# Logarithm and scans of the forget gates ordered behind the evictions of the forgetting attention, and spread over one more step of the fill

## The chip, the core and the metric

The kernel runs on one core of a Trainium2 chip. The metric is device time in microseconds (us). TensorE (PE) multiplies, with its weight loads on PEld; VectorE (DVE), ScalarE (ACT) and GpSimd (POOL) work element by element; SyncE (SP) issues most of the transfers.

## The reference

One residual block on a sequence of 1024 rows of 1024 elements, in float32. After a norm and one input projection three mixers run side by side: HGRN2 (a gated linear recurrence, 4 heads with 128 x 128 states), the forgetting attention (8 heads of 64) and cross-attention into a memory. Their outputs are projected, gated, summed and projected again; a ConvGLU channel mixer follows. What the change touches is the decay of the HGRN2 heads:

```python
f = lb + (1.0 - lb) * jax.nn.sigmoid(f_logit.astype(jnp.float32))
kh = heads(1.0 - f)
G = jnp.cumsum(heads(jnp.log(f)), axis=3)      # within chunks of 64 rows
...
o = (jnp.einsum('bhts,bhsv->bhtv', A, ic)      # A: queries, keys and exp of differences of G
     + jnp.einsum('bhtc,bhcv->bhtv', qc * jnp.exp(Gc), S))
```

The forgetting attention, beside which this work runs, is per head and block of 128 queries

```python
s = (jnp.einsum('bhqd,bhkd->bhqk', qh[:, :, lo:hi], kh[:, :, :hi]) * scale
     + Fc[:, :, lo:hi, None] - Fc[:, :, None, :hi])
p = jax.nn.softmax(jnp.where(mask, s, -jnp.inf), axis=-1)
outs.append(jnp.einsum('bhqk,bhkd->bhqd', p, vh[:, :, :hi]))
```

## The kernel before

All large products are run as three matmuls each (`mm3`, lines 110 to 112): high part by high part, low by high, high by low. The projections that the mixers need later are not done in one piece. A generator, `fill_steps()`, deals them out: 18 units of `cm_unit`, each with 7 yields (products of sums of blocks, so that 7 products stand for 8), and 24 chunks of the branch projections behind them. Six steps run alone, and then the generator is woven with the eight heads of the forgetting attention (`fox_attn(h)`, about 330 to 690 us, with 2, 6 and then 5 steps of the fill to a head, `FOX_FILL`), with the four HGRN heads (`hgrn_mix(h)`), and the rest runs out behind them. The fill gives PE work while the attention waits for its softmax.

A unit of the fill loads weights into `ur` (SP, L798), forms sums `us` on POOL (L738), casts them to the high part `uh` on ACT (L732), takes the low part `ul` on DVE (L733), multiplies into `pp`, copies results out on ACT (`ue`, L743), combines them on DVE (`ue` and `uo`, L136, L138, L784) with activations on ACT (L763, L773, L776, L783), and stores to DRAM.

A head of the attention has four groups `tp`. Each takes two blocks of queries: logits `lg` by PE (L1029, L1030), a masked sum with a row maximum on DVE (L1035), the negated maximum (L1042), exp on ACT (L1045), reciprocal on DVE (L1046), scaling on POOL (L1047). Then PE transposes the probabilities into `tr` (L1058 to L1061), they are split into `ph` (a cast on ACT, L116) and `pl` (a subtraction on DVE, L124), and PE multiplies them with the values into `po` (L1070, L1071). `po` is emptied by a copy of its upper half on ACT (`yp`, L1074) and an add of the lower half on DVE (L1075), and `yp` is stored (L1076). There are 32 such evictions. The next head's inputs (`kh`, `qa`, `kl`, `nf`, `vhl`: L999 to L1005, on SP) are loaded behind the first `yp` store of the head before.

`decays(h)` makes the decays of HGRN head `h`: load of the gate into `fk` (SP, L949), two tensor_scalars on DVE (L952, L953), the logarithm of 128 x 2048 elements on ACT (L955), with a load of its table ahead of it and of exp's or tanh's table again ahead of the next activation, four scans (L958) and four subtractions (L959) of 128 x 256 on DVE, and two stores (L962, SP). `fk` has one buffer, so a load waits for the stores of the head before. `fill_steps` calls it in units 1, 2, 4 and 5: the load at step 2, all the computation at step 4, the stores at step 6.

What sets the order: a scheduler puts the instructions of each engine into one order when the program is built, by priorities and its own estimate of when each can run; the attention's have a priority raised by `AHEAD`. Inside `tc.issue_after(x)` an instruction comes to stand behind instruction `x` in the order of its own engine. That adds no wait; each engine then runs strictly in its order. `marks["cast"]` is the last cast of a `uh` so far, `marks["head"]` the first `yp` store of a head.

Of the kernel before, what the change touches and what calls it, by code (L numbers as in the profile page):

```python
# [12 lines left out]
ALU = mybir.AluOpType  # L13
# [55 lines left out]
def tile_block(ctx: ExitStack, tc: tile.TileContext, xT, x_rows, memT, mem_rows, vec, fbias, mats, hmask, w_ff, w_tm, w_cm,  # L69
               w_mkv, w_br, w_out, w_up, w_dn, outT):  # L70
    nc = tc.nc
    V, S, G, PE, SP = nc.vector, nc.scalar, nc.gpsimd, nc.tensor, nc.sync
# [655 lines left out]
    marks = {}  # L728
# [59 lines left out]
    def cm_unit(u, puts):  # L788

        x, z, y = (banks[(u + i) % 3] for i in range(3))  # L790

        def put(c, n, ps, e):
            puts[c](c, n, ps, e)

        raw = []
        for i in range(4):
            t = ur.tile([P, HB], F32, tag="ur", name="ur", bufs=4)
            SP.dma_start(t, w_cm[u, i])  # L798
            raw.append(t)
        a11, a12, a21, a22 = raw  # L800
        o1, o6 = u_operand(a11), u_operand(a12)
        s1 = u_sum(a21, a22)
        s2 = u_sum(s1, a11)
        u_product(x, o1, "B11", True)
        e1 = u_snap(x)
        yield
        u_product(z, o6, "B21", True)
        put(0, 0, z, e1)
        o3 = u_operand(s2)
        yield  # L810
        u_product(x, o3, "T2", False)
        e2 = u_snap(x)
        o2 = u_operand(s1)
        s4 = u_sum(s2, a12)
        yield
        u_product(y, o2, "T1", True)
        e5 = u_snap(y)
        o5 = u_operand(u_sum(a11, a21))
        yield
        u_product(x, o5, "T3", False)  # L820
        put(1, 1, x, e5)
        o4 = u_operand(s4)
        yield
        u_product(y, o4, "B22", False)
        put(0, 1, y, e2)
        o7 = u_operand(a22)
        yield
        u_product(x, o7, "T4", False)
        put(1, 0, x, None)
        yield  # L830

    def puts_of(what, i):
        return put_gate(i) if what == "gt" else put_hg("fqg".index(what), i)
# [95 lines left out]
    def load_y(br):  # L929
        yr[br] = [fam_tile(("B11", "B22")[ORDER.index(br) % 2], p, (P, 2, T), F32) for p in "hl"]  # L930
        for i, t in enumerate(yr[br]):
            n = 2 if br or i == 0 else 1
            SP.dma_start(t[:, :n, :], yd3[br][:, 2 * i:2 * i + n, :])
# [12 lines left out]
    def decays(h):  # L946

        fk = pf.tile([P, 2, T], F32, tag="fk", name=f"fk_{h}")
        SP.dma_start(fk[:, 0, :], hgd[h][0])  # L949
        yield  # L950
        hc = slice(h, h + 1)
        V.tensor_scalar(fk[:, 1, :], fk[:, 0, :], nc1[:, hc], c1p[:, hc], ALU.mult, ALU.add)  # L952
        V.tensor_scalar(fk[:, 0, :], fk[:, 0, :], c1[:, hc], c0[:, hc], ALU.mult, ALU.add)  # L953
        with tc.issue_after(marks["cast"].ins):
            S.activation(fk, fk, AF.Ln)  # L955
        for n in range(4):
            sl = slice(n * 256, (n + 1) * 256)
            V.tensor_tensor_scan(fk[:, 0, sl], resets, fk[:, 0, sl], 0.0, ALU.mult, ALU.add)  # L958
            V.tensor_sub(fk[:, 1, sl], fk[:, 0, sl], fk[:, 1, sl])  # L959
        yield  # L960
        for i in range(2):
            SP.dma_start(hgd[h][3 + i], fk[:, i, :])  # L962

    def fill_steps():
        for u, spec in enumerate(UNITS):
            for i, _ in enumerate(cm_unit(u, [puts_of(*s) for s in spec])):
                if u == len(UNITS) - 1 and i == 1:
                    load_y(ORDER[0])
                if u == 3 and i == 4:
                    recurrence_masks()  # L970
                if u in (1, 2, 4, 5):
                    if i == 2:
                        steps = decays((1, 2, 4, 5).index(u))
                    if i in (2, 4, 6):
                        next(steps, None)
                yield
        yield from branches()
        ur.release()
# [10 lines left out]
    resets = pf.tile([P, 256], F32, tag="resets", name="resets")  # L989
# [20 lines left out]
    def fox_attn(h):  # L1010
        p, a = h // 2, slice(64 * (h % 2), 64 * (h % 2) + 64)
        with tc.issue_after(marks["head"].ins) if h else nullcontext():
            kh, kl, qa, vhl, nf = fox_load(h)
        for tp in range(4):
            pts = []
            for j in range(2):
                tb = 2 * tp + j
                ns = (tb + 1) * P
                tsl = slice(tb * P, (tb + 1) * P)
                pt = pf.tile([P, T], F32, tag="pt", name="pt", bufs=4)  # L1020
                st = pf.tile([P, 4], F32, tag="st", name="st", bufs=4)
                nfm = pf.tile([P, P], F32, tag="nfm", name="nfm")
                G.tensor_tensor(nfm, nf[tb // 4][:, tb % 4 * P:tb % 4 * P + P], mskf, ALU.add)
                m = 0
                for s0 in range(0, ns, HB):
                    w = min(HB, ns - s0)
                    ps = ps_lg()
                    with tc.issue_after(begun.ins):
                        PE.matmul(ps[:, :w], qa[:, tsl], kh[:, s0:s0 + w], start=True, stop=False)  # L1029
                    PE.matmul(ps[:, :w], qa[:, tsl], kl[:, s0:s0 + w], start=False, stop=True)  # L1030

                    d = w - P if s0 + w == ns else w
                    for lo, hi, bias in ((0, d, nf[s0 // HB][:, :d]), (d, w, nfm)):
                        if lo < hi:
                            V.tensor_tensor_reduce(out=pt[:, s0 + lo:s0 + hi], in0=ps[:, lo:hi], in1=bias,  # L1035
                                                   op0=ALU.add, op1=ALU.max, scale=1.0, scalar=-3e38,
                                                   accum_out=st[:, m:m + 1])
                            m += 1
                if m == 3:
                    V.tensor_tensor(st[:, 0:1], st[:, 0:1], st[:, 2:3], ALU.max)  # L1040
                if m > 1:
                    V.tensor_scalar(st[:, 2:3], st[:, 0:1], st[:, 1:2], -1.0, ALU.max, ALU.mult)  # L1042
                else:
                    V.tensor_scalar(st[:, 2:3], st[:, 0:1], -1.0, None, ALU.mult)
                S.activation(pt[:, :ns], pt[:, :ns], AF.Exp, bias=st[:, 2:3], accum_out=st[:, 3:4])  # L1045
                V.reciprocal(st[:, 3:4], st[:, 3:4])  # L1046
                G.tensor_scalar(pt[:, :ns], pt[:, :ns], st[:, 3:4], 0.0, ALU.mult, ALU.add)  # L1047
                pts.append(pt)
                yield
            po = ps_po()  # L1050
            for sp in range(tp + 1):
                ptr = ps_tr()
                w = 384 if sp == tp else 512
                for jj in range(2):
                    sb = 2 * sp + jj
                    ssl = slice(sb * P, (sb + 1) * P)
                    if sb <= 2 * tp:
                        PE.transpose(ptr[:, jj * 256:jj * 256 + P], pts[0][:, ssl], ident)  # L1058
                        PE.transpose(ptr[:, jj * 256 + P:jj * 256 + 256], pts[1][:, ssl], ident)
                    else:  # L1060
                        PE.transpose(ptr[:, 256:384], pts[1][:, ssl], ident)  # L1061
                ph = pf.tile([P, HB], F32R, tag="ph", name="ph", bufs=2)
                pl = pf.tile([P, HB], F32R, tag="pl", name="pl", bufs=2)
                split(S, ph[:, :w], pl[:, :w], ptr[:, :w])
                for jj in range(2):
                    sb = 2 * sp + jj
                    last = sb == 2 * tp + 1
                    o = po[:, P:256] if last else po[:, 0:256]
                    src = slice(256, 384) if last else slice(jj * 256, jj * 256 + 256)
                    PE.matmul(o, vhl[:, sb, :], ph[:, src], start=(sb == 0), stop=False)  # L1070
                    PE.matmul(o, vhl[:, sb, :], pl[:, src], start=False, stop=last)  # L1071
                yield
            yp = pf.tile([64, 256], F32, tag="yp", name="yp")
            S.copy(yp, po[64:128, :256])  # L1074
            V.tensor_add(yp, po[0:64, :256], yp)  # L1075
            stored = SP.dma_start(yd3[1][a, p, tp * 256:(tp + 1) * 256], yp)  # L1076
            if tp == 0:
                marks["head"] = stored
            yield
# [592 lines left out]
    for a, b, own, first, c, n, sign, last, xq in (  # L1672
# [9 lines left out]
        for i, ks in enumerate(steps):  # L1682
# [11 lines left out]
            for m in range(4):  # L1694
                w = 256 if end and ks.stop == NP and m == 3 else HB
                for t0 in range(0, HB, w):
# [7 lines left out]
                    if ks.stop == NP:  # L1704
                        j, sl = m + 4 * c, slice(n * HB + t0, n * HB + t0 + w)
# [105 lines left out]
```

## Time and profile before

| | |
|---|---|
| runs | 1704.29, 1705.58, 1708.75 us; median 1705.58 |
| profiled execution | 1707.61 us, its span 1705.8 |
| mean granted TensorE clock | 0.992 |
| PE busy | 1673.9 us, 98% of the span |
| DVE, ACT, POOL busy | 1214.6, 844.5, 449.1 us |

A busy PE is the bound almost everywhere, so the profile is read for the few microseconds in which PE stands, what ended each of them, and what that instruction had been queued behind on its own engine. Rows of the trace give the start, the duration, the engine, the line of the kernel, the operation, output <- input, the shape, and in brackets the idle time of the engine just before with what ended it. The four logarithms of the decays start at 340.3, 374.9, 427.5 and 458.8 us.

### The profile page before, as it was taken

How to read it: one execution, taken by the hardware profiler on the slowest of the kernel's cores; microseconds unless marked ns; L12 is line 12 of the kernel's file. 1: busy time of each engine (PE TensorE's matmuls, PEld its weight loads, DVE VectorE, ACT ScalarE, POOL GpSimd, SP SyncE). 2: the span in 40 equal slices, each digit the busy share in tenths (PEclk: the TensorE clock that was granted, in tenths of full speed). 3: DMA queues.
4: the chain of work that ended last, by engine and by line, in shares of the span. 5: the costliest groups of instructions: out<-in, count | busy, mean ns of one | idle time of the engine just before them, and what ended most of it. 6: DMA issues, size and time to landing. Idle time of an engine off the chain costs nothing. (4 is left out here: it accounts for less than half of the span.)

```text
span 1705.8 us, 24936 instructions
## 1 busy us (share of the span) xinstructions
PE 1673.9 (98%) x8883; PEld 1414.9 (83%) x8883; DVE 1214.6 (71%) x2177; ACT 844.5 (50%) x1449; POOL 449.1 (26%) x482
## 2 busy tenths in 40 slices
PE   8999999999899999999999999999999999999999
PEld 5989999778788888888888787888888888788887
DVE  7875765587876666789676667878778777674654
ACT  7745554466666655565332357434444334343331
POOL 0333543565454543222111224211111111100000
PEclk9999999999999999999999999999999999999999
DMA  7353352656555542557858998756345454394772
GB/s 288 111 186 104 126 189 93 227 176 178 182 146 161 149 133 93 189 165 259 281 180 224 282 250 188 220 152 164 117 130 149 135 144 140 138 378 138 258 253 87
DMA packets 134749, 305.54 MB, mean 179 GB/s; under 512 B 14328, under 2 KB 31992, under 8 KB 133984
## 3 DMA queue, kind: packets, MB, share of 16 engines
q1 hardware_dynamic: 101008, 210.87, 36.8%
q0 software_dynamic: 24400, 78.39, 18.3%
q10 hardware_dynamic: 9216, 14.68, 2.4%
q8 instruction: 70, 1.15, 0.3%
q14 instruction: 55, 0.45, 0.1%
HBM read 223.21 MB, written 107.41 MB: 194 GB/s over the span
## 5 line engine op out<-in xcount | busy, mean ns | idle before, releaser
L1348 ACT CAST wh<-s 128x512 fp32r<-128x512 f32 x80 | 48.8, 618 | 120.3 <-PE pp L111 65.2
L116 ACT CAST dwh<-wr 128x1024 fp32r<-128x1024 f32 (+1 forms) x41 | 40.1, 978 | 119.0 <-PE tr L111 40.4
L1348 ACT CAST wh<-rw 128x512 fp32r<-128x512 f32 x70 | 43.1, 620 | 90.0 <-PE pp L111 48.4
L732 ACT CAST uh<-ur 128x512 fp32r<-128x512 f32 x78 | 48.2, 618 | 77.4 <-PE pp L111 65.1
L1473 POOL DMA_DIRECT2D rw<-in_w_up x40 | 22.0, 556 | 199.9 <-DVE wl L1349 151.9
L1047 POOL TENSOR_SCALAR pt<-pt,st 128x128 f32<-128x128 f32 (+3 forms) x64 | 57.2, 895 | 60.0 <-DVE st L1046 42.4
L124 DVE TENSOR_TENSOR dwl<-wr,dwh 128x1024 fp32r<-128x1024 f32 (+1 forms) x41 | 46.3, 1129 | 37.1 <-ACT dwh L116 37.1
L110 PE MATMUL pp<-B21h,uh 128*128 128x512 f32 x168 | 67.0, 400 | 4.1 <-DVE gt L897 2.9
L1045 ACT ACTIVATE pt<-pt,st 128x128 f32<-128x128 f32 (+3 forms) x64 | 49.8, 778 | 40.6 <-DVE st L1042 34.9
L733 DVE TENSOR_TENSOR ul<-us,uh 128x512 fp32r<-128x512 f32 x72 | 54.4, 760 | 17.4 <-ACT uh L732 17.0
L112 PE MATMUL pp<-B21h,ul 128*128 128x512 f32 x168 | 66.5, 396 | 0.1
L111 PE MATMUL pp<-T2l,uh 128*128 128x512 f32 x168 | 66.5, 396 | 0.0
L112 PE MATMUL pp<-T2h,ul 128*128 128x512 f32 x168 | 66.4, 396 | 0.0
L110 PE MATMUL pp<-T2h,uh 128*128 128x512 f32 x168 | 66.4, 399 | 0.0
L111 PE MATMUL pp<-B21l,uh 128*128 128x512 f32 x168 | 66.3, 394 | 0.0
L733 DVE TENSOR_TENSOR ul<-ur,uh 128x512 fp32r<-128x512 f32 x78 | 59.6, 765 | 8.6 <-ACT uh L732 8.6
L738 POOL TENSOR_TENSOR us<-ur 128x512 f32<-128x512 f32 x36 | 49.9, 1386 | 58.3 <-DMA ur<-in_w_cm 49.3
L1349 DVE TENSOR_TENSOR wl<-rw,wh 128x512 fp32r<-128x512 f32 x70 | 46.9, 684 | 20.9 <-PE pp L112 16.7
L738 POOL TENSOR_TENSOR us<-us,ur 128x512 f32<-128x512 f32 x36 | 51.0, 1416 | 40.5 <-issue 34.9
L124 DVE TENSOR_TENSOR wl<-raw,wh 128x1024 fp32r<-128x1024 f32 x29 | 37.1, 1284 | 31.9 <-ACT wh L116 31.7
L732 ACT CAST uh<-us 128x512 fp32r<-128x512 f32 x72 | 43.8, 614 | 32.0 <-POOL us L738 16.1
L1349 DVE TENSOR_TENSOR wl<-s,wh 128x512 fp32r<-128x512 f32 x80 | 54.5, 681 | 0.0
(721 smaller groups left out, 6161.9 us busy)
## 6 DMA issues: line engine op xcount, KB each, us to landing
rw<-in_w_up POOLq DMA_DIRECT2D x40, 512.0 KB, 4.7
ur<-in_w_cm SPq DMA_DIRECT2D x72, 256.0 KB, 3.8
sd<-in_w_dn POOLq DMA_DIRECT2D x30, 512.0 KB, 5.9
br<-yd SPq DMA_DIRECT2D x30, 512.0 KB, 4.7
gd<-uo ACTq DMA_DIRECT2D x48, 256.0 KB, 2.4
gt<-gd SPq DMA_DIRECT2D x48, 256.0 KB, 6.2
yd<-fc SPq DMA_DIRECT2D x44, 256.0 KB, 2.1
raw<-in_w_tm SPq DMA_DIRECT2D x20, 512.0 KB, 3.8
```

Source lines behind the costliest of these rows:

```text
L110: PE.matmul(ps, lh, rh, start=first, stop=False, skip_group_check=more)
L111: PE.matmul(ps, lh, rl, start=False, stop=False, skip_group_check=more)
L112: return PE.matmul(ps, ll, rh, start=False, stop=last, skip_group_check=more)
L116: S.copy(out, in_)
L124: return (sub or V).tensor_sub(l, src, h.bitcast(F32))
L732: marks["cast"] = S.copy(h, src)
L733: V.tensor_sub(l, src, h.bitcast(F32))
L738: G.tensor_add(t, a, b)
L1045: S.activation(pt[:, :ns], pt[:, :ns], AF.Exp, bias=st[:, 2:3], accum_out=st[:, 3:4])
L1047: G.tensor_scalar(pt[:, :ns], pt[:, :ns], st[:, 3:4], 0.0, ALU.mult, ALU.add)
L1348: late["cast"] = S.copy(h, src)
L1349: late["split"] = V.tensor_sub(l, src, h.bitcast(F32))
```

## The change

In `decays` the computation is cut by two more yields: tensor_scalars, then the logarithm with the first two scans and subtractions, then the other two. `fill_steps` now advances it at each step from 2 on, so that the load is at step 2, the tensor_scalars at 3, the logarithm and half of the scans at 4, the other half at 5, the stores at 6. The logarithm is ordered on ACT behind the last copy of `yp` that has been written so far (`marks["out"][0]`) in place of the last cast; the scans and subtractions are ordered on DVE behind the last add of `yp` (`marks["out"][1]`), where nothing held them before. Lines behind the diff's places move by up to 3: the logarithm is L956, scans and subtractions L960 and L961, the stores L965, exp L1048, copy and add of `yp` both L1077, its store L1078.

```diff
@@ decays
         V.tensor_scalar(fk[:, 0, :], fk[:, 0, :], c1[:, hc], c0[:, hc], ALU.mult, ALU.add)
-        with tc.issue_after(marks["cast"].ins):
+        yield
+        with tc.issue_after(marks["out"][0].ins):
             S.activation(fk, fk, AF.Ln)
         for n in range(4):
             sl = slice(n * 256, (n + 1) * 256)
-            V.tensor_tensor_scan(fk[:, 0, sl], resets, fk[:, 0, sl], 0.0, ALU.mult, ALU.add)
-            V.tensor_sub(fk[:, 1, sl], fk[:, 0, sl], fk[:, 1, sl])
-        yield
+            with tc.issue_after(marks["out"][1].ins):
+                V.tensor_tensor_scan(fk[:, 0, sl], resets, fk[:, 0, sl], 0.0, ALU.mult, ALU.add)
+                V.tensor_sub(fk[:, 1, sl], fk[:, 0, sl], fk[:, 1, sl])
+            if n % 2:
+                yield
@@ fill_steps
-                    if i in (2, 4, 6):
+                    if i >= 2:
                         next(steps, None)
@@ fox_attn
-            S.copy(yp, po[64:128, :256])
-            V.tensor_add(yp, po[0:64, :256], yp)
+            marks["out"] = (S.copy(yp, po[64:128, :256]), V.tensor_add(yp, po[0:64, :256], yp))
```

The instructions are the same ones; their order differs on every engine from the first logarithm (340 us) to about 980 us. Three places, with numbers at names for buffers (`fk_5884` is the third head's `fk`, `fk_4238` and `fk_4779` the first and second head's).

ACT before, around the third head's logarithm, which runs at 427.5 us:

```order
L732 CAST uh<-us 128x512
L743 COPY ue<-pp 128x512
L955 ACT_TABLE_LOAD
L955 ACTIVATE fk_5884<-fk_5884 128x2048
L1074 COPY yp<-po 64x256
L116 CAST ph<-tr 128x512 x2
L732 CAST uh<-ur 128x512
```

ACT in the changed kernel, around the first head's logarithm, ahead of which 7 copies of `yp` stand now and none stood before:

```order
L1048 ACTIVATE pt,st<-pt,st 128x256
L1077 COPY yp<-po 64x256
L956 ACT_TABLE_LOAD
L956 ACTIVATE fk_4238<-fk_4238 128x2048
L783 ACT_TABLE_LOAD
L783 ACTIVATE uo<-ue 128x512
L116 CAST ph<-tr 128x512 x2
```

The copy of `yp` now stands ahead of the logarithm, and the casts of `ph` behind it. At all four heads it is so; ahead of the second, third and fourth logarithm stand 12, 23 and 28 copies now, and stood 2, 6 and 9.

DVE before, the third head's decays and the add of `yp`:

```order
L952 TENSOR_SCALAR fk_5884<-fk_5884,nc_180,c1p 128x1024
L1046 RECIPROCAL st<-st 128x1
L953 TENSOR_SCALAR fk_5884<-fk_5884,c_176,c_175 128x1024
L733 TENSOR_TENSOR ul<-us,uh 128x512
L958 SCALAR_TENSOR_TENSOR fk_5884<-resets,fk_5884 128x256 x4
L1075 TENSOR_TENSOR yp<-po,yp 64x256
L959 TENSOR_TENSOR fk_5884<-fk_5884 128x256
```

DVE in the changed kernel, the third head's scans behind one add of `yp` (the other two stand 26 rows further on, behind the next add):

```order
L1077 TENSOR_TENSOR yp<-po,yp 64x256
L960 SCALAR_TENSOR_TENSOR fk_5884<-resets,fk_5884 128x256 x2
L124 TENSOR_TENSOR pl<-tr,ph 128x512
L961 TENSOR_TENSOR fk_5884<-fk_5884 128x256 x2
L124 TENSOR_TENSOR pl<-tr,ph 128x512
```

The add stands ahead of the scans now. At the third and fourth head the scans are in two halves; at the first and second head all four stand in one row behind one add.

SP before, between the second head's stores and the next head's inputs:

```order
L962 DMA hgd_79<-fk_4779 128x1024 x2
L785 DMA hgd_79<-uo 128x512
L1076 DMA yd_88<-yp 64x256
L785 DMA hgd_79<-uo 128x512
L798 DMA ur<-in_w_cm 128x512 x3
```

SP in the changed kernel, the same stores:

```order
L1078 DMA yd_88<-yp 64x256
L965 DMA hgd_79<-fk_4779 128x1024 x2
L798 DMA ur<-in_w_cm 128x512
L949 DMA fk_5884<-hgd_80 128x1024
L1078 DMA yd_88<-yp 64x256
L1002 DMA kh_5352<-kqd_72 64x1024
```

The load of the third head's `fk` now follows the second head's stores at once, and a head's inputs stand right behind.

## The prediction

> **What bounds the kernel now.** I read the busy time first, then TensorE (PE) by stretches, then the list of PE's waits, and last the places where these waits lie. The page's head:
>
> ```profile
> span 1705.8 us, 24936 instructions
> PE 1673.9 (98%) x8883; PEld 1414.9 (83%) x8883; DVE 1214.6 (71%) x2177; ACT 844.5 (50%) x1449; POOL 449.1 (26%) x482
> ```
>
> PE is busy for 98% of the span and the change takes no matmul away, so only what lies between the matmuls, or slows them, can be won. Busy time of each engine in five stretches of the forgetting attention (columns: stretch, length, PE, PEld, DVE, ACT, POOL, granted clock, DMA share, GB/s):
>
> ```profile
> 370.00:410.00 40.00, 37.49 (x194) 30.60 (x193) 34.91 (x94) 26.55 (x50) 23.43 (x22) 1.00 0.44 149
> 410.00:450.00 40.00, 34.92 (x173) 29.29 (x172) 27.06 (x73) 23.58 (x45) 22.70 (x25) 0.91 0.54 159
> 450.00:500.00 50.00, 49.79 (x267) 41.92 (x266) 41.35 (x114) 33.59 (x63) 20.50 (x25) 1.00 0.57 174
> 500.00:560.00 60.00, 60.00 (x329) 51.44 (x328) 40.07 (x123) 35.83 (x74) 27.51 (x33) 1.00 0.57 164
> 560.00:620.00 60.00, 60.00 (x328) 51.35 (x327) 41.14 (x127) 36.81 (x77) 27.02 (x33) 1.00 0.42 126
> ```
>
> PE loses 2.5 us in the first and 5.1 us in the second, and nothing from 500 to 620, where DVE works 67% of the time against 87% in the first. The whole-span list of PE's waits (waiter, releaser: total, times, longest) says for what:
>
> ```profile
> PE po L1070 <- DVE yp L1075: 4.3, 1, 4.3
> PE pp L110 <- DVE gt L897: 2.9, 1, 2.9
> PE lg L1030 <- DMA kl<-kqd: 1.5, 2, 0.8
> ```
>
> The longest wait is the attention's, for the DVE add that empties `po`. PE around it:
>
> ```profile
> 427.45 0.39 PE L111 MATMUL pp<-T3l,uh 128*128 128x512 f32 x1
> 427.68 0.39 PE L112 MATMUL pp<-T3h,ul 128*128 128x512 f32 x1
> 432.34 0.55 PE L1070 MATMUL po<-ph,vhl 128*128 128x256 f32 x1 [4.28 <-DVE yp L1075]
> 432.69 0.63 PE L110 MATMUL pp<-B22h,uh 128*128 128x512 f32 x1
> 433.12 0.63 PE L111 MATMUL pp<-B22l,uh 128*128 128x512 f32 x1
> 437.38 0.54 PE L112 MATMUL pp<-B22h,ul 128*128 128x512 f32 x1
> ```
>
> Starts are 0.23 us apart before the wait and 0.43 us after it. Twelve matmuls run so slowly (432.69 to 437.38), which adds 12 x 0.20 = 2.4 us to the 4.28: this wait cost 6.7 us. ScalarE (ACT), then DVE, in the same stretch:
>
> ```profile
> 424.90 1.28 ACT L955 ACT_TABLE_LOAD   x1
> 427.50 1.91 ACT L955 ACTIVATE fk<-fk 128x2048 f32<-128x2048 f32 x1 [1.32 <-DVE fk L953]
> 429.44 0.37 ACT L1074 COPY yp<-po 64x256 f32<-64x256 f32 x1
> 432.44 1.28 ACT L776 ACT_TABLE_LOAD   x1
> ```
> ```profile
> 425.81 0.81 DVE L952 TENSOR_SCALAR fk<-fk,nc,c1p 128x1024 f32<-128x1024 f32 x1 [2.55 <-DMA fk<-hgd]
> 429.45 2.44 DVE L958 TENSOR_TENSOR_SCAN fk<-resets,fk 128x256 f32<-128x256 f32 x4 [1.38 <-ACT fk L955]
> 431.80 0.39 DVE L1075 TENSOR_TENSOR yp<-po,yp 64x256 f32<-64x256 f32 x1
> ```
>
> This is the third head's decays. DVE waits for the load of `fk`, ACT waits for DVE, `yp`'s copy stands behind the logarithm, and its add behind four scans: the eviction of `po` ends some 4 us later than its matmuls.
>
> **What the change removes.** It runs no instruction less. It turns the order round: copy and add of `yp` come first, the logarithm and the scans behind them. On ACT 7, 12, 23 and 28 copies of `yp` now stand ahead of the four logarithms, where it was 0, 2, 6 and 9. The first comes about when the third did; the other three leave 340 to 465 us for the stretches in which PE hardly waited. PE's other gaps in the old place, and the first one behind the fourth logarithm, which starts at 458.8:
>
> ```profile
> 347.10 0.50 PE L112 MATMUL pp<-B11h,ul 128*128 128x512 f32 x1 [0.45 <-DVE ul L733]
> 372.75 0.50 PE L110 MATMUL pp<-T4h,uh 128*128 128x512 f32 x1 [0.26 <-DVE ue L136]
> 381.77 0.47 PE L110 MATMUL pp<-B21h,uh 128*128 128x512 f32 x1 [1.22 <-DVE ue L138]
> 386.42 0.33 PE L1058 MATMUL tr<-ident,pt 128*128 128x128 f32 x1 [0.75 <-DVE pl L124]
> 474.25 0.33 PE L1058 MATMUL tr<-ident,pt 128*128 128x128 f32 x1 [0.21 <-POOL pt L1047]
> ```
>
> I charge the first four to the decays, since the DVE result that PE lacked was queued behind their instructions: 0.45 + 0.26 + 1.22 + 0.75 = 2.7 us. With the 6.7 that is 9.4 us. The two waits for `kl` (1.5 us together, in the list above) are loads of heads 1 and 2. On SyncE (SP) they stood behind stores of `fk` that waited for DVE; these stores are gone from there, so 1.5 more can come back. Removed: 10.9 us at most. Less than all of it goes if something else was nearly as late at these places; below nothing it cannot be, since the work really leaves them.
>
> **What it adds: the logarithm behind the copy.** In the new order the split's cast of `ph`, which feeds the next `po`, stands behind a table load (1.28) and the logarithm (1.91): 3.2 us, and 4.5 us at the first head, where the reload (1.28) stands before the cast as well. On DVE the scans (2.44 for four) wait for the logarithm, with the subtraction `pl` behind them. Two things hide it: the fill's matmuls between one group of `po` and the next, and that PE's own input lies in `uh` and `ul` ahead of it. What this is worth per head is bounded by the same instructions in the old places: at most 0.21 us after the fourth logarithm (the row at 474.25, which a softmax's scaling ended), 1.22 + 0.75 = 2.0 us after the second. I take 0.6 each, nearer the low row, because the new places lie where DVE has a third of its time free; 4 x 0.6 = **2.4 us**, bounds 0 and 8. If the cover is gone the price is that of the 432 row.
>
> [...] This case's rows on ACT around the first logarithm:
>
> ```profile
> 338.81 0.19 ACT L1045 ACTIVATION_READ_ACCUMULATOR pt<-pt,st 128x1 f32 x1
> 339.01 1.28 ACT L955 ACT_TABLE_LOAD   x1
> 340.31 1.92 ACT L955 ACTIVATE fk<-fk 128x2048 f32<-128x2048 f32 x1
> ```
>
> [...]
>
> **What it adds: the chain of stores and loads.** `fk` is one buffer. The second, third and fourth head's load stands on SP right behind the stores of the head before (one load of `ur` between them), and DVE's next tensor_scalar (L952) stands some 16 to 24 rows behind the last subtraction. From the waits of DVE between 335 and 470 us, and the landing times of the stores (L962) and of the loads (L949):
>
> ```profile
> DVE fk L952 <- DMA fk<-hgd: 6.6, 3, 2.6
> ```
> ```profile
> L962 SPq DMA_DIRECT2D hgd<-fk x8: 320/326/327, 345.8 to 464.7; - x8
> DMA to landing us min/median/max: 2.6/4.7/6.9
> ```
> ```profile
> L949 SPq DMA_DIRECT2D fk<-hgd x4: 319/320/325, 332.3 to 449.5; - x4
> DMA to landing us min/median/max: 3.7/4.4/5.1
> ```
>
> Store and load need 4.7 + 4.4 = 9.1 us, with the extremes 6.3 to 12.0. The rows that DVE has for that time (for the second head three `ul` at 0.7, two `pl`, three softmax reductions and small ones) come to about 6 us. So DVE stands some 3 us at each of three places, 0 to 6; in the trace it stood three times for 2.5 us. One of these cost PE 0.26 (the row at 372.75), the other was a part of the 4.28. I take 0.7 each, nearer the first since no eviction hangs on this wait any more: **2.0 us**, with 0 and 6.7 a head as the bounds.
>
> **Queues and the tail.** The head loads of the third head wait on SP no more, but those of the heads behind a block of decays do: the stores wait for the last subtraction, and the next `yd` store and `kh`, `qa`, `kl` stand behind. I price it as one of the two `kl` waits, **0.7 us**, bounds 0 and 1.5. Last, the order also differs further on, up to about 980 us: some 9 us more of the fill's matmuls now run under the attention, and so less is left beside the recurrence. There the trace has
>
> ```profile
> 948.49 0.50 PE L110 MATMUL pp<-B21h,uh 128*128 128x512 f32 x1 [2.92 <-DVE gt L897]
> 950.00:955.00 5.00, 5.00 (x16) 3.94 (x16) 5.00 (x8) 2.61 (x3) 0.88 (x1) 0.69 1.06 323
> ```
>
> a wait for a gate that came late, with the DMA engines full (share 1.06) and the clock at 0.69 behind it, about 1.5 us (5 x 0.31) more. It can vanish or come twice: 4.4 us either way. I take **0.3 us** as a loss.
>
> **Sum.** 10.9 - 2.4 - 2.0 - 0.7 - 0.3 = 5.5 us. The profiled execution took 1707.61 us (1.8 outside its span), so 1702.1 for a run like it; it stood 2.03 above the median of 1705.58, so **1700.1 us** beside that median, 0.32% less.
>
> **Rivals.** *No change: the waits only move.* A logarithm still costs 3.2 us of ACT and 2.4 us of scans, wherever it stands, and at heads 1 and 2 all four scans still follow each other in one block: dealing them out over two steps shows only at heads 3 and 4. With four logarithms at the high end near 1.5 us and the waits for `fk` at 1.5 us, 6.0 + 4.5 + 1.0 stand against 10.9: 1706.2. For it: the second logarithm did cost 2.0. Against it: DVE had no free time there and has it at the new places.
>
> *The whole gain.* If every new wait is hidden, 10.9 us come back: 1694.7. For it: the 120 us from 500 on in which PE did not stop once. Against it: the order in those stretches is another one now, and the work that is added there was not in it.
>
> *Slower: the one buffer of* `fk`. At L952 all of DVE's queue stands behind one DMA chain: `ul` for the fill, `pl` for `po`, the softmax reductions. If the chain takes its long end (6.9 + 5.1 = 12.0 us against 6 us of cover), DVE stands 6 us, and once PE has run through what lies ready it stands longer than 2.9 us and comes back at the low clock, as at 432 and 948. Each such place costs up to the 6.7 us of the 432 row instead of 0.7. One of them leaves 1706.1; it decides from two on: 1712.1. Against it: 6.9 is the extreme of eight stores, and the DMA share is 0.57 or less in the new stretches. [...]
>
> *Slower: the tail.* One more wait like that at 948 with its clock, 4.4 us, and nothing gained there, on top of the first rival: 1710.6.
>
> **How the numbers follow.** The forecast has 0.52, with 1697 to 1703 as its own range; no change 0.20; the whole gain 0.13; `fk` 0.10; the tail 0.05. Around this kernel's runs 0.3%, or 5.1 us, is what can be told from no change. The forecast lies just beyond that bound: I put 0.33 of its 0.52 beyond it and 0.19 within. With the whole gain, faster has 0.46; same has 0.19 + 0.19 = 0.38; slower 0.10 + 0.05 + 0.01 from the first rival's upper end = 0.16. The range reaches from below the whole gain, 1693, to 1709, which leaves out the two slower cases nearly whole and little else.
>
> **What would show it.** Right: no wait of PE for `yp` over 1 us; from 370 to 450 us PE busy some 79 of 80 us at clock 1.00; behind the four new logarithms, gaps of PE under 1 us each; waits of DVE for `fk` near 3 us with under 1 us of PE behind each. Wrong: a gap over 2.9 us behind an L952 or behind a logarithm with matmuls 0.43 us apart; PE waiting for `kl` for more than 1.5 us in all; or a longer stretch from 900 to 1000 us than the 97.0 of 100 busy now.

## The result, and the profile after

The changed kernel takes 1716.53 us (median of 9 runs, 1711.89 to 1720.88) beside 1706.19 us for the kernel before (9 runs, 1702.63 to 1708.75). The ratio is 1.0055 with a 95% interval of 1.0043 to 1.0066: about 9.4 us **slower**, where 5.5 us faster was forecast and 1709 was the upper end of the range. Its profiled execution took 1711.92 us, near the fast end of its own runs; a second profiled execution took 1716.42 us (span 1714.6) and shows most of the same waits, some of them longer.

The page's head:

```profile
span 1710.1 us, 24938 instructions
PE 1672.3 (98%) x8883; PEld 1411.7 (83%) x8883; DVE 1213.5 (71%) x2177; ACT 842.6 (49%) x1449; POOL 456.1 (27%) x482
```

The same work, 4.3 us longer. Four of the five stretches of the attention that the prediction showed, now; from 500 to 560 us PE is full, as before (columns: stretch, length, PE, PEld, DVE, ACT, POOL, granted clock, DMA share, GB/s):

```profile
370.00:410.00 40.00, 40.00 (x215) 33.82 (x214) 29.34 (x84) 21.06 (x43) 17.71 (x20) 1.00 0.48 139
410.00:450.00 40.00, 36.33 (x180) 29.99 (x181) 30.84 (x83) 25.28 (x48) 25.58 (x26) 0.96 0.48 148
450.00:500.00 50.00, 49.49 (x264) 41.76 (x263) 39.15 (x110) 34.84 (x65) 20.43 (x23) 1.00 0.57 181
560.00:620.00 60.00, 59.55 (x322) 50.71 (x321) 41.80 (x119) 38.00 (x72) 26.68 (x29) 1.00 0.47 144
```

From 370 to 450 us PE is busy 76.3 of 80 us against 72.4 before, at a clock of 0.96 against 0.91 in the second half. Between these two profiles there is a gain, though less than the 79 us at clock 1.00 that the prediction named. The stretches behind the attention, of before and then of the changed kernel, which the prediction hardly looked at:

```profile
700.00:800.00 100.00, 100.00 (x607) 85.23 (x606) 91.23 (x176) 61.48 (x121) 28.77 (x23) 1.00 0.61 201
800.00:840.00 40.00, 39.95 (x226) 33.90 (x226) 30.40 (x67) 17.80 (x38) 4.88 (x6) 1.00 0.89 317
900.00:1000.00 100.00, 96.96 (x424) 78.67 (x423) 67.98 (x92) 37.72 (x52) 21.03 (x24) 0.98 0.95 254
1000.00:1100.00 100.00, 97.14 (x422) 78.80 (x421) 74.20 (x111) 62.63 (x99) 35.53 (x45) 0.97 0.84 205
```
```profile
700.00:800.00 100.00, 98.64 (x575) 82.58 (x574) 87.66 (x170) 60.30 (x119) 23.30 (x21) 1.00 0.63 214
800.00:840.00 40.00, 37.50 (x224) 31.76 (x223) 27.14 (x60) 14.51 (x32) 3.74 (x5) 1.00 0.93 301
900.00:1000.00 100.00, 96.36 (x426) 77.97 (x425) 63.65 (x90) 34.63 (x50) 23.87 (x27) 0.98 0.92 247
1000.00:1100.00 100.00, 94.94 (x413) 76.55 (x412) 75.06 (x109) 65.59 (x105) 35.59 (x45) 0.97 0.85 214
```

PE was full from 700 to 840 us and now stands 1.4 and 2.5 us there, and 2.2 more between 1000 and 1100. The list of PE's waits of the changed kernel from 400 to 1075 us:

```profile
PE pp L110 <- DVE gt L897: 3.2, 2, 2.6
PE po L1412 <- DMA r<-sq: 2.6, 1, 2.6
PE tr L1204 <- ACT kT L1201: 2.5, 1, 2.5
PE po L1074 <- DVE pl L124: 2.0, 2, 1.4
PE po L1073 <- ACT ph L116: 1.7, 1, 1.7
PE pp L110 <- DVE r L1328: 1.7, 1, 1.7
PE lg L1032 <- DVE ul L733: 1.5, 1, 1.5
```

The wait for `yp` is gone. Three rows belong to the change's new places in the attention (`pl`, `ph`, `ul`), two are new and far behind it (`kT` in the recurrence at 810 us, and the wait for `r` from DVE, L1328, in the output projection at 1053), and two were there before (`gt` and `r<-sq`, 2.9 us each).

For the comparison of many profiles I use one measure, **PE's lost time**: for each matmul the time to the start of the next one, less what quick pairs of the same two shapes take in these profiles (the 20th percentile over them). It holds idle time and a low clock alike. In us, by stretch:

| | 320-480 | 480-680 | 680-800 | 800-880 | 880-1100 |
|---|---|---|---|---|---|
| before | 22.5 | 8.1 | 3.8 | 2.6 | 15.5 |
| changed, first profile | 14.9 | 11.5 | 6.1 | 5.3 | 18.9 |
| changed, second profile | 14.2 | 12.4 | 6.6 | 7.5 | 18.9 |

Against this one profile of before, the attention (320 to 680) gained 4.0 to 4.2 us. Behind it 8.4 and 11.1 us were lost. (The first 320 us, which no edit touches, scatter from 23 to 28 us between profiles, so a difference of 2 us between two whole profiles says nothing by itself.)

The attention scatters too, and the profile of before stands at the high end. In the four control runs further down, which are the kernel before with an edit behind the attention, PE runs in the order of before up to 826 us at least, and they lost about 27 to 29.5 us from 320 to 680. Seven profiles with the changed order lost about 26 to 28. By the means, 29 and 27 us, the gain is nearer 2 us than 4. The wait at 432 us explains most of it: 4.28 us in the profile of before, with a granted clock of 0.50 over the twelve matmuls behind it (432.69 to 437.38 us), it was 2.5 to 2.7 us in the four controls. The row of the control with the eight transfers early:

```profile
433.04 0.36 PE L1070 MATMUL po<-ph,vhl 128*128 128x256 f32 x1 [2.57 <-DVE yp L1075]
```

### The profile page after: what moved, and what is told of

Same layout as the page of the kernel before. It is cut to its first block, busy times and chain, and to the rows that moved or that the text cites. A ratio compares the mean times of both kernels' runs of the same rounds, so it can differ in the third digit from the quotient of the medians.

```text
span 1710.1 us, 24938 instructions
## 1 busy us (share of the span) xinstructions
PE 1672.3 (98%) x8883; PEld 1411.7 (83%) x8883; DVE 1213.5 (71%) x2177; ACT 842.6 (49%) x1449; POOL 456.1 (27%) x482
## 5 line engine op out<-in xcount | busy, mean ns | idle before, releaser
L732 ACT CAST uh<-ur 128x512 fp32r<-128x512 f32 x78 | 48.0, 617 | 50.1 <-PE pp L111 32.3
L110 PE MATMUL pp<-B21h,uh 128*128 128x512 f32 x168 | 67.5, 402 | 3.2 <-DVE gt L897 3.2
L733 DVE TENSOR_TENSOR ul<-ur,uh 128x512 fp32r<-128x512 f32 x78 | 63.2, 812 | 9.0 <-ACT uh L732 8.1
L1048 ACT ACTIVATE pt<-pt,st 128x128 f32<-128x128 f32 (+3 forms) x64 | 49.8, 778 | 38.3 <-DVE st L1045 30.1
L110 PE MATMUL pp<-T2h,uh 128*128 128x512 f32 x168 | 66.4, 397 | 0.0
L112 PE MATMUL pp<-T2h,ul 128*128 128x512 f32 x168 | 66.4, 396 | 0.0
L112 PE MATMUL pp<-B21h,ul 128*128 128x512 f32 x168 | 66.2, 395 | 0.0
L1050 POOL TENSOR_SCALAR pt<-pt,st 128x128 f32<-128x128 f32 (+3 forms) x64 | 51.6, 807 | 52.2 <-DVE st L1049 37.5
L1026 POOL TENSOR_TENSOR nfm<-nf,mskf 128x128 f32<-128x128 f32 x64 | 39.4, 616 | 62.5 <-DVE st L1038 49.7
```

The source lines that it names most:

```text
L110: PE.matmul(ps, lh, rh, start=first, stop=False, skip_group_check=more)
L112: return PE.matmul(ps, ll, rh, start=False, stop=last, skip_group_check=more)
L732: marks["cast"] = S.copy(h, src)
L733: V.tensor_sub(l, src, h.bitcast(F32))
```

## The experiments

**Two theories.** *Attention*: the new waits at the logarithms eat the gain. *Tail*: the attention gains, and the loss lies behind 680 us, because the recurrence's heads come later against the fill and its transfers. In the changed kernel 3886 matmuls of `mm3` (L110 to L112) stand ahead of the last product with `kT` in the recurrence, 3838 before, so 48 more of the fill; the copies of `kT`, two for each head, show the delay in time (before, then changed):

```profile
L1199 ACT COPY kT<-tr x8: 478/525/594, 703.0 to 895.0; 128x512 f32<-128x512 f32 x4, 128x384 f32<-128x384 f32 x4
```
```profile
L1201 ACT COPY kT<-tr x8: 470/526/588, 708.4 to 907.0; 128x512 f32<-128x512 f32 x4, 128x384 f32<-128x384 f32 x4
```

The first copy is 5.4 us late, the last one 12.0.

### The changed kernel again

> The changed kernel once more, for a second profile and on one chip with the runs beside it. Its first profile is 4.3 us longer than the one of before, its median 10 us. Both theories: about 1.0055 of before (1.004 to 1.007). The attention theory (the new waits inside the attention, 330 to 700 us, make the loss) expects this profile to have lost its time before 700 us. The tail theory (the attention gains some 4 us, and the loss lies behind 700 us, where the recurrence's heads stand 9 to 12 us later against the fill) expects PE's lost time from 320 to 680 us to be 3 to 5 us below that of before and that from 680 to 1100 us 7 to 13 us above it.

1717.95 us, 1.0058 (1.0044 to 1.0073). Lost time from 320 to 680 us is 4.0 below the profile of before, from 680 to 1100 us 11.1 above: the tail theory's numbers.

### Which edit acts

```diff
-        with tc.issue_after(marks["cast"].ins):
+        with tc.issue_after(marks["out"][0].ins):
             S.activation(fk, fk, AF.Ln)
```

> Kernel before with one edit of the three: the logarithm ordered behind the last copy of yp. No order for the scans, no additional step. The order that comes out is that of the changed kernel up to about 617 us and differs between there and about 750 us. If the logarithm's place is all that acts: 1.0055 within 0.002, like the changed kernel. If the order of the scans or the additional step makes the loss: 1.000 or below.

1.0043 (1.0027 to 1.0058), and in the profile the changed kernel's pattern: 26.5 us lost in the attention, 34.3 behind it. The logarithm's place is what acts. The instruction order of programs that were built but not run confirms it for the rest: to order the scans as well gives exactly the order of this kernel on every engine, so that edit moves nothing; the additional step alone, without the two orders, moves a handful of rows on DVE and SyncE and none on PE. Beside the logarithm's edit the step does move PE's rows between about 600 and 750 us, but the two ratios, 1.0043 and 1.0055, have overlapping intervals.

### One head's logarithm at a time

Each is the kernel before with this edit for the heads named (0 is the first):

```diff
-        with tc.issue_after(marks["cast"].ins):
+        with tc.issue_after((marks["out"][0] if h == 2 else marks["cast"]).ins):
```

> Kernel before with the logarithm of the third head alone ordered behind the copy of yp. The order is that of before up to about 425 us and again from about 667 us on, so the whole tail stands as before. Tail theory: the 6.7 us of the 432 wait come back less 1 to 3 us for the new place, and behind 700 us nothing is lost: 1700 to 1703 beside 1706 (0.997 to 0.999). Attention theory: the new place costs as much as the old one gave, 1705 to 1709 (0.999 to 1.002).

> Kernel before with the logarithm of the fourth head alone ordered behind the copy of yp. The first three heads stay as before, with the 4.3 us wait of PE at 432 us; the recurrence's last head stands behind 3882 matmuls of the fill, against 3838 before and 3886 in the changed kernel. Tail theory: the tail's loss comes without the gain, 7 to 12 us slower (1.004 to 1.007). Attention theory: one logarithm in a calm place costs 0 to 1 us, so 1.000 within 0.001.

> Kernel before with the logarithm of the first head alone ordered behind the copies of yp; 7, 7, 10 and 10 copies now stand ahead of the four logarithms (0, 2, 6 and 9 before). The recurrence's last head stands behind 3829 matmuls of the fill (3838 before, 3886 in the changed kernel). Tail theory: lost time behind 680 us within 2 us of before (21.9 us), so the time is set by the attention, with the first head's wait behind the logarithm (3 us) and logarithms that crowd: 0.998 to 1.002. Any-rearrangement theory: 1.002 or more, with 4 us or more lost behind 680 us.

| moved | ratio (95%) | 320-480 | 480-680 | 680-1100 | `mm3` ahead of the last product with `kT` |
|---|---|---|---|---|---|
| none | 1 | 22.5 | 8.1 | 21.9 | 3838 |
| third | 1.0022 (1.0010 to 1.0033) | 16.0 | 15.5 | 20.4 | 3838 |
| fourth | 1.0038 (1.0023 to 1.0052) | 22.0 | 9.8 | 29.0 | 3882 |
| first | 1.0026 (1.0012 to 1.0041) | 23.7 | 8.9 | 25.5 | 3829 |
| all (changed) | 1.0055 (1.0043 to 1.0066) | 14.9 | 11.5 | 30.2 | 3886 |

The fourth head alone is the clearest: one logarithm in a calm place costs 0.4%, with the loss behind 680 us, as the tail theory said and the attention theory did not. The third head alone took the wait at 432 away (PE at 400 to 440 us, below: 2.4 us lost there, 9.2 in the profile of before), and lost 7 us again near 620, where the fourth head's `fk` and the next head's inputs now follow its stores. The third head's kernel, stretches and PE's waits there:

```profile
400.00:440.00 40.00, 39.25 (x212) 33.53 (x211) 31.05 (x92) 22.53 (x47) 23.37 (x24) 1.00 0.53 153
600.00:640.00 40.00, 35.72 (x178) 28.91 (x176) 28.98 (x90) 25.87 (x47) 23.18 (x22) 0.96 0.58 184
...
PE lg L1030 <- DMA kl<-kqd: 1.9, 1, 1.9
PE lg L1029 <- DMA qa<-kqd: 1.3, 1, 1.3
```

So both of my numbers for its time were off: I had the stall removed and no new one. Its 0.22% is not in its profile, whose execution was the shortest of its 11 runs; what those longer runs lost stays open. The first head alone has 9 matmuls fewer ahead of the last product with `kT`, but in its profile the recurrence still ends later than before (last copy of `kT` at 900.5 us against 895.0), and it loses 3.6 us behind 680, between the numbers of the two theories. 3 of them lie between 800 and 880, where PE waits 2.5 us once for the recurrence's state (`St`, from DVE) and not for `kT`: the count of matmuls ahead does not tell by itself what will collide.

> Kernel before with the logarithms of the third and fourth head ordered behind the copies of yp (23 and 28 copies ahead of them, as in the changed kernel), the first two as before. The order behind 720 us is that of before. Tail theory: the 6.7 us of the wait at 432 come back, 2 to 4 us are lost near 600 to 660 us as in the changed kernel, nothing behind 720 us: 0.997 to 0.999. Any-rearrangement-costs theory: 1.002 or more, as with the third head alone (1.0022).

> Kernel before with the logarithms of the first and second head ordered behind the copies of yp; 7, 12, 13 and 14 copies ahead of the four. The recurrence's last head stands behind 3834 matmuls of the fill, as before. Tail theory: 4 us come back from 360 to 400 us and 2 to 6 at 432, the third and fourth head's chain of stores and loads costs 3 to 8 near 500 us, nothing is lost behind 680 us: 0.997 to 1.000. Any-rearrangement theory: 1.002 or more.

> Kernel before with the logarithms of the first and fourth head ordered behind the copies of yp; 7, 7, 10 and 28 copies ahead of the four. The recurrence stands as in the run with the third and fourth head (last head behind 3838 matmuls). Tail theory: behind 680 us within 3 us of before; in the attention 4 us less near 360 to 400 us and 3 us more at the first logarithm's new place: 0.997 to 1.001. Any-rearrangement theory: 1.002 or more.

Third and fourth: 1.0012 (1.0003 to 1.0021), 31.2 us lost in the attention (30.6 before), 22.2 behind it. First and fourth: 1.0009 (0.9997 to 1.0021), 32.3 and 18.6. First and second: 1.0015 (1.0003 to 1.0027), 27.2 and 28.7. None gains, and the ratios of the third and fourth and of the first and second lie above the range of the tail theory. Where the recurrence stands as before (PE's order is that of before from 723 us on), little or nothing is lost behind 680 us, but the attention loses 31 to 32 us: its waits move from 432 to 450 or to 620. It falls to 27 only where the first two heads' logarithms are both moved, and there 7 us were lost behind it, against my expectation that nothing would be.

### The wait at 810 us

In the changed kernel's second profile, SyncE's issues, then ScalarE, then PE:

```profile
797.08 0.32 SPq L933 DMA_DIRECT2D B22l<-yd  x1
797.49 0.38 SPq L933 DMA_DIRECT2D B22h<-yd  x1
...
799.91 0.45 SPq L846 DMA_DIRECT2D ur<-in_w_br  x1
```
```profile
812.32 0.62 ACT L732 CAST uh<-ur 128x512 fp32r<-128x512 f32 x1 [8.56 <-DMA ur<-in_w_br]
...
813.34 0.47 ACT L1201 COPY kT<-tr 128x384 f32<-128x384 f32 x1
```
```profile
813.86 0.94 PE L1204 MATMUL tr<-hi,kT 128*128 128x128 f32 x6 [3.38 <-ACT kT L1201]
```

Two tiles of 1 MB for the second branch go out ahead of a branch weight; ScalarE stands 8.6 us at that weight's cast, and the recurrence's copy of `kT`, whose input is ready, stands behind the cast. In the kernel before that copy comes ahead of the burst (793.4 us against 802.4). The experiment holds the two tiles back, in the changed kernel and as a control in the kernel before:

```diff
-                if i == 0:
-                    load_y(ORDER[1])
             if i == 14:
                 load_y(ORDER[2])
             load_gates(i)
+            if i == 3:
+                with tc.issue_after(marks["gate"].ins):     # the last load of a gate
+                    load_y(ORDER[1])
```

> The changed kernel with the load of the second branch's inputs (two tiles of 1 MB each, issued on SyncE at 795 us) held back behind the gates of the fourth chunk. If PE's wait for kT at 810 us (2.3 to 3.4 us in three profiles) comes from a branch weight that lands late behind these 2 MB, while ScalarE stands at its cast with the copy of kT queued behind: the wait goes below 1 us, and the time falls by 2 to 4 us (1.0035 to 1.0045) unless the transfers come in the way later. If not: the wait stays over 2 us.

> The control to the run that held the second branch's inputs back: the same edit in the kernel before, where no wait stands near 800 to 840 us (1.4 us of lost time there). If the edit takes away a clash that only the late recurrence makes: 1.000 within 0.001, no gain. If loading these inputs later is better by itself: 0.998 or below, as the changed kernel gained some 0.25%.

Changed: 1.0034 (1.0021 to 1.0048), some 3.6 us better, with intervals that just overlap. The wait is gone, and PE is full from 800 to 840 us:

```profile
800.00:840.00 40.00, 40.00 (x240) 34.35 (x239) 27.72 (x60) 15.28 (x33) 3.46 (x5) 1.00 0.86 276
```

Control: 0.9997 (0.9987 to 1.0007). In the kernel before, the burst costs nothing that can be told.

> The kernel with the first and second head's logarithms behind the copies of yp (attention 3.4 us better in its profile, 1.0015 of before because of 6.8 us lost behind 680 us) and with the second branch's inputs held back as in the run that gained 4 us in the changed kernel. If the waits near 790 us (4.9 us in the windows from 760 to 800) have the same cause: they go, and 0.997 to 0.9995. If not: 1.0015 stays.

The same edit on the first and second head's kernel: 1.0016 (1.0004 to 1.0029), no gain. Its 4.8 us between 760 and 800 us stayed at 4.1, so they have another cause.

### The transfers behind 900 us

GpSimd issues the sums of the up weights in DRAM behind the norm of the recurrence's last half. The first of them, before and changed:

```profile
L921 POOL DMA_DIRECT2D ud<-in_w_up x4: 1312/1340/1376, 914.8 to 916.9; - x4
```
```profile
L921 POOL DMA_DIRECT2D ud<-in_w_up x4: 1305/1330/1371, 926.6 to 928.7; - x4
```

They start 11.8 us later and meet the loads of the output projection's weights. From 900 to 940 us the core moves less than before (198 against 222 GB/s), and then the DMA engines are full (share 1.04 to 1.06 from 940 to 1020 us in both kernels) and little is caught up: 293 GB/s against 285 from 940 to 980 us, 248 against 246 from 980 to 1020. Before, changed:

```profile
900.00:940.00 40.00, 39.89 (x185) 32.66 (x184) 27.56 (x42) 12.48 (x20) 9.68 (x11) 1.00 0.80 222
```
```profile
900.00:940.00 40.00, 40.00 (x194) 33.42 (x192) 29.69 (x47) 12.82 (x23) 10.42 (x12) 1.00 0.71 198
```

First attempt: all eight transfers behind the last half but one.

```diff
-    with tc.issue_after(marks["last"].ins):
+    with tc.issue_after(marks["early"].ins):     # the norm of the half before
         run_all(up_sums())
```

> The changed kernel with one more edit: the eight transfers that sum the up weights in DRAM, which GpSimd issues behind the norm of the recurrence's last half, stand behind the norm of the half before it. The order of the other engines up to 920 us stays. So far: in all kernels whose recurrence ends 12 to 16 us late, PE lost 7 to 12 us more behind 680 us, the last weight sums start 12 us later, and 1.7 to 2.8 MB less were moved from 860 to 940 us. If the late transfers make the loss behind 940 us: the start of these transfers moves from 926 to about 902 us, PE's waits from 940 to 1060 us shrink by 3 to 6 us, 1.002 to 1.004 of before. If they do not: 1.0055 within 0.001. The losses near 705 and 810 us (4 to 5 us) stay in both.

> The same edit in the kernel before, as the control. If the late transfers explain the difference between the two kernels, it gains less here than there: 0 to 3 us, 0.998 to 1.000. If it gains as much or more than in the changed kernel, the crowd of transfers is common to both and does not explain the difference.

1.0069 (1.0055 to 1.0083) and 1.0036 (1.0022 to 1.0050): both slower, and the edit is to blame. GpSimd in the changed kernel with it:

```profile
902.31 3.39 POOL L921 DMA_DIRECT2D ud<-in_w_up  x4
914.95 1.16 POOL L923 DMA_DIRECT2D ud<-in_w_up  x1 [9.25 <-DMA ud<-in_w_up]
...
933.90 1.32 POOL L129 TENSOR_TENSOR rr<-rr,mhalf 128x4 f32<-128x4 f32 x1
```
```profile
PE tr L1115 <- ACT o L1112: 8.4, 1, 8.4
```

The additions wait for the copies to land, the last half's norm (`rr`) stands behind them on GpSimd, and PE waits 8.4 us for what hangs on it (7.3 in the kernel before with this edit). These two runs say nothing on the crowd. Second attempt, with less to move: the four additions left out.

```diff
-        for i, b in ((0, up(2)), (3, up(1)), (1, ud[:, 0]), (2, ud[:, 1])):
-            yield G.dma_start(ud[:, i], b, accum_op=ALU.add)
```

> The changed kernel without the four transfers that add the second summand to the up weights' sums in DRAM (left out: those additions, so the channel mixer's weights are incomplete). They are issued on GpSimd between 937 and 968 us, in the stretch in which the DMA engines are full (share 1.05). If the crowd of transfers makes the loss behind 880 us: lost time of PE from 880 to 1100 us falls from 19 to 12 to 15 us, and it falls by 2 us more than in the kernel before with the same edit; 1.003 of before or below. If the order of the engines makes it: 19 us stay within 2, 1.005.

> The kernel before without the same four transfers (same part left out), as the control: crowd theory, lost time from 880 to 1100 us from 15.5 to 11 to 14 us, 0.998 to 0.9995; order theory, 15.5 within 1.5 us and 1.000.

Changed: 1.0014 (0.9999 to 1.0028), lost time from 880 to 1100 us from 18.9 to 11.8. Before: 0.9978 (0.9964 to 0.9992), from 15.5 to 10.6. The difference between the kernels there falls from 3.4 to 1.2 us, as the crowd theory expected. Single profiles prove little here, though: with one and the same order of PE from 723 us on, four profiles (before, third, third and fourth, first and fourth) lost from 11.2 to 15.5 us in this stretch. The times say the same, 0.0041 gained against 0.0022, with intervals that leave it short of certain. Third attempt, with all the work done: the four copies early, the additions where they were.

```diff
+    up_parts = up_sums()
+    with tc.issue_after(marks["early"].ins):
+        for _ in range(4):
+            next(up_parts)
     with tc.issue_after(marks["last"].ins):
-        run_all(up_sums())
+        run_all(up_parts)
```

> The changed kernel with only the four copies of the up weights' sums (GpSimd, 926.6 to 928.7 us) moved behind the norm of the recurrence's last half but one (about 902 us); the additions stay. Crowd theory: no new wait of the last norm, lost time of PE from 880 to 1100 us falls from 19 to 13 to 17 us, 1.002 to 1.0045 of before. Order theory: 19 within 2, 1.0055 within 0.001.

> The same in the kernel before, as the control. Crowd theory: it has the crowd too, but 12 us earlier and less of it: lost time from 880 to 1100 us from 15.5 to 12 to 15.5 us, 0.998 to 1.000, a smaller gain than in the changed kernel. Order theory: 1.000 within 0.001.

> The changed kernel with both repairs: the second branch's inputs held back (it gave 4 us) and the four copies moved forward. If the two losses are apart, their repairs add up: 1.0034 less 0.001 to 0.0025, so 1.001 to 1.0025. It beats the kernel before only if what is left behind 680 us is under the 4 us that the attention gained.

Changed: 1.0036 (1.0023 to 1.0049), lost time from 880 to 1100 us 14.8. Before: 1.0007 (0.9994 to 1.0019), 13.9 in its profile and no gain in time. With both repairs the changed kernel comes to 1.0006 (0.9996 to 1.0017), a little below the range that I expected: they add up, the interval lies clear of the changed kernel's (1.0043 to 1.0066), and no difference to the kernel before can be told any more. PE's waits from 780 to 1075 us in that kernel:

```profile
PE po L1419 <- DMA r<-sq: 3.1, 1, 3.1
PE po L110 <- ACT T4h L116: 1.8, 1, 1.8
PE pp L110 <- DVE gt L898: 1.6, 3, 0.8
```

The wait for `kT` is gone, and so is the 1.7 us wait for `r` from DVE; the wait for `r<-sq`, which the kernel before has too (2.9 us), stays. Its attention lost 26.2 us (30.6 in the profile of before), 680 to 800 us 6.1 (3.8), the rest behind 800 us 17.8 (18.1). So no version that does all the work beats the kernel before.

## Why the prediction was wrong

**What failed: the term for the tail.** It stood in the sum as a loss of 0.3 us, 4.4 either way, and as a rival with a chance of 0.05. The trace of the changed kernel lost 8 to 11 us there. I had seen that 9 us more of the fill run under the attention, but priced only one known wait (948 us) for it. What I did not follow is what hangs on the recurrence's end: the first copy of `kT` 5 us late, the last 12 us, the weight sums behind it 12 us. Two of the three pieces are shown by a repair and its control: some 3.6 us at 810 us (ratio 1.0055 to 1.0034, control unchanged, and the wait gone from the trace) and some 3 us from 880 us on (1.0055 to 1.0036, control unchanged). Each step alone is near the edge of what can be told; both together, 1.0055 to 1.0006, are clear of it. The third piece, 2.3 to 2.8 us between 680 and 800 us, was not tested; the rows there are waits for `uo`, `ue` and the recurrence's `kE`.

**What is removed** was right in kind and too large in size. The wait at 432 went (from 9.2 to 2.4 us lost between 400 and 440 us, where only the third head moved), the stretch from 360 to 400 us lost 1.6 instead of 6.1, and no wait for `kl` is in the list. But the 6.7 us were the price of one execution: in the four controls that wait was 2.5 to 2.7 us, and they lost 5.0 to 6.7 us between 400 and 440 us in place of 9.2. In the changed kernel that stretch still lost 7.8 us, for the first logarithm has come to stand there.

**The logarithm behind the copy** was priced at 0.6 us a head, 2.4 in all. The rows are 1.73 + 1.40 at the first head and 0.45, 0.45 and 0.58 at the others, 4.6 us. The first head is the mis-sized one:

```profile
414.87 0.37 ACT L1077 COPY yp<-po 64x256 f32<-64x256 f32 x1
415.26 1.28 ACT L956 ACT_TABLE_LOAD   x1
416.55 1.92 ACT L956 ACTIVATE fk<-fk 128x2048 f32<-128x2048 f32 x1
418.49 1.28 ACT L783 ACT_TABLE_LOAD   x1
419.78 0.63 ACT L783 ACTIVATE uo<-ue 128x512 f32<-128x512 f32 x1
420.43 1.07 ACT L116 CAST ph<-tr 128x512 fp32r<-128x512 f32 x2
```
```profile
421.07 0.38 PE L1073 MATMUL po<-ph,vhl 128*128 128x256 f32 x1 [1.73 <-ACT ph L116]
422.85 0.39 PE L1074 MATMUL po<-pl,vhl 128*128 128x256 f32 x1 [1.40 <-DVE pl L124]
```

Behind these two gaps the clock is low (from 424.0 to 427.4 us, the column before the last two):

```profile
424.00:427.40 3.40, 3.40 (x13) 2.91 (x12) 3.40 (x10) 1.10 (x3) 0.30 (x1) 0.50 0.85 283
```

By my estimate half of these 3.4 us, 1.7 us, come on top: 6.3 us in place of 2.4, still inside the bounds of 0 and 8. The cast of `ph` comes 5.2 us behind the copy's end (420.43 against 415.24), with the reload and one activation ahead of it, and `pl` behind the scans adds its own wait. I had counted 4.5 us on ScalarE and trusted the fill to cover it. At most 0.02 us stands on either side of a table load there (415.24 to 415.26, 416.54 to 416.55).

**The chain of stores and loads** was right. DVE waited 3.0, 1.5 and 2.6 us at the three loads where I put 3 each, and PE paid 1.46 us behind the last of them (the `ul` row) where I put 2.0 in all. In this profile no queue of loads cost PE anything that can be told; in the second PE waited 0.98 us for `qa` at 628 us, where I had 0.7 in all. With the forecast sizes the attention alone was to be 5.8 us better; it came out 4.1 better against the profile of before, and some 2 us by the means of all profiles. That, and a tail that lost 8 to 11 us, is near the 9.4 us that were measured.

**Rivals.** The slower one that I gave the chance to, the one buffer of `fk`, did not decide: PE stood under 1.5 us behind each of those waits. The rival that came true is the tail, at half its size in my text, and a chance of 0.05 was too low for an edit that makes the scheduler place some 11 us of matmuls (48 at 0.23 us) elsewhere. It also stood on top of the first rival, in which the attention gains nothing, and that part did not come true.

## What to carry over

An edit to one engine's order in a program that a scheduler packs moves whatever comes behind it. Before trusting a local gain, follow the milestones behind it (the end of each later stage, the first issue of each bulk transfer) in the new order, and ask which transfers are tied to them. Price a collision by finding what stands next to a burst of transfers on each queue, not by the waits that the old order happened to have. Take the size of a wait from more than one execution before it enters a sum: the largest term here rested on a 4.28 us wait that was 2.5 to 2.7 us in four others. And when stalls are repaired one at a time, look for where the queue stops next: here the 432 us wait went to 450 or 620 us.

## What was not expected of the hardware

The clock did not fall at one length of a gap. In one execution of the changed kernel (first profile) a gap of 2.50 us left the clock alone (granted 1.00 from 805 to 825 us), and one of 2.55 us was followed by matmuls 0.43 us apart (granted 0.67 from 960 to 965 us):

```profile
810.80 0.94 PE L1204 MATMUL tr<-hi,kT 128*128 128x128 f32 x6 [2.50 <-ACT kT L1201]
811.49 0.48 PE L110 MATMUL pp<-B21h,uh 128*128 128x512 f32 x1
```
```profile
959.60 0.54 PE L110 MATMUL pp<-B21h,uh 128*128 128x512 f32 x1 [2.55 <-DVE gt L897]
959.94 0.63 PE L111 MATMUL pp<-B21l,uh 128*128 128x512 f32 x1
960.37 0.63 PE L112 MATMUL pp<-B21h,ul 128*128 128x512 f32 x1
```

In the run with the logarithm's edit alone matmuls 0.43 us apart followed a gap of 2.10 us (granted 0.82 from 810 to 815 us, 0.83 from 815 to 820), and at the first logarithm (rows above) they followed two gaps of 1.73 and 1.40 us (granted 0.50 from 424.0 to 427.4 us). I had put the point at 2.9 us. The granted clock in the trace of the changed kernel's first profile shows more: it stands at half from 424.02, 959.91 and 1058.90 us on, for one or two times 3.413 us, and these starts are 157 and 29 such steps apart. On the grid of these three starts, which I carry on as an estimate to the places between them, the gap of 2.55 us lies whole inside the step that ends at 959.91, while an edge at 809.73 cuts the gap of 2.50 us into 1.43 and 1.07 us. Both gaps are shorter than a step. That their place on the grid made the difference is my reading of these rows; no run tested it.
